# SSD decay built with log dt and a mask added on GpSimd, and projection slabs placed elsewhere, in a hybrid trunk layer

## Chip, cores and metric

One Trainium2 chip, one core. The metric is the device time of one execution of the whole layer, in microseconds, lower is better.

## The reference, cut to what matters

One layer over 256 context tokens and 1024 latent tokens of width 1024: modulated RMSNorm, an input projection whose columns go to three mixers (SSD, gated MLP, S5), an output projection, then a squared-ReLU MLP. The change touches the chunked SSD and the order of the projections:

```python
xbc = silu(conv5(s[..., XBC]))                 # columns x (512), B (2x128), C (2x128)
dt  = softplus(s[..., DT] + dt_bias)           # per direction and head
a_cum = cumsum(dt * a, chunk axis)             # chunks of 128 tokens
seg  = a_cum[q] - a_cum[k]
lmat = exp(where(k <= q, seg, -inf))           # reversed in the backward direction
y_diag = einsum(C[q] . B[k], lmat, x[k] * dt[k])
y_off  = einsum(C, h_prev, exp(a_cum))
h = chunk_decay * h + einsum(B, decay_to_end, x * dt)   # from chunk to chunk
y = y_fwd + y_bwd + d * x;   y = rmsnorm(y * silu(z))
```

## The kernel before, in words

Everything is float32 with channels on the partitions. Products with weights are done as three matmuls (`mm3`, L219 to L221) on high and low halves; a weight slab of 1024 x 128 (`wslab`) is loaded, split by ScalarE and VectorE, and multiplied with the token tiles of 256, 512 and 512 columns: 24 steps, 72 matmuls a slab. The slabs of interest: `xbc_slab(m)`, eight of them, each followed by a five-tap convolution (ScalarE's first tap, four `stt` on VectorE over 1284 columns, tanh, and a last multiplication on VectorE for m in 0, 1, 4, 6 and on GpSimd for the others) and stored to `xbc_d`; `u_slab`, two, a Gelu and a store issued from ScalarE's queue; `z_slab`, four, a Tanh, an `stt` and a store.

In the order of the source: input norm, the v/dt and S5 input projections, `sgu_mix`, two u slabs; then the S5 part, eight groups (`s5_main`), which holds five PSUM banks (`psA`); then xbc slabs 0, 1, 4, 6, `dt_chain`, and `psA.close()`. The SSD part takes the same banks as `psB`, so it starts when S5 is through. It has two head groups. `right()` walks the chunks from the last to the first and keeps the backward state of each (`hb`); `outputs()` walks forward over ten chunks. Group 0 needs slabs 0, 1, 4, 6; group 1 needs 2, 3, 5, 7, which stand between `right0` and `out0`. `right1` goes beside the last chunks of `out0`; z slabs 0 and 1 and `s5_glu` stand between `out0` and `out1`; z slabs 2 and 3, two `mixed_tile` and the first output slabs go beside `out1`.

A chunk of `outputs()` (L882 to L937): `rb`, the cumulated decay as rows for 4 heads and 2 directions, is broadcast from DRAM (three buffers); ScalarE makes `er = exp(rb)`; then the decay matrix is made head by head with pairs of a ScalarE and a VectorE instruction (`rb<-rb,col`), its minimum with the other direction and one Exp over 512 columns; `tok_major` transposes the chunk and C.B goes to `pcb`; VectorE masks `pcb` with both triangles (`cm`), four ScalarE and four VectorE instructions weigh it by dt (`rb<-cm,DTD`), and a VectorE product over 512 columns gives the operand of the matmuls at L918. State matmuls (L925) follow, `er`, `cm` and the store to `y_d` close the chunk, and `new_state` (L854) carries `hf` on.

The tile framework orders the instructions of each engine before the run with a planner: source order is the priority, and an instruction whose inputs and buffers are there may go ahead of earlier ones that are not ready. Each engine, and each DMA queue, then runs its list strictly in that order.

## Time and profile before

| what | value |
|---|---|
| median of 3 runs | 1580.24 us (1580.15 to 1582.12) |
| the profiled execution | 1578.67 us, span 1576.7 us |
| TensorE busy over the span | 1423.4 us (90%) |
| VectorE, ScalarE, GpSimd busy | 1067.9, 751.1, 389.5 us |
| granted TensorE clock, mean | 0.947 |

A granted clock of 1.00 is the upper level (2.4 GHz), 0.5 the lower (1.2 GHz); a mean between them is a mixture in time. Times of the rows are microseconds from the start of the span, durations of one instruction nanoseconds.

### The profile page before, as it was taken

What the parts mean: (1) busy time and instruction counts of PE and PEld (TensorE: products, weight loads), DVE (VectorE), ACT (ScalarE), POOL (GpSimd) and SP (SyncE); (2) the same over time, 40 slices, a digit from 0 to 9 for tenths busy, and PEclk for the clock granted to TensorE, in tenths of its full rate; (3) what the DMA queues carried; (4) which work ended last, traced back from release to release, by engine and by line L of the source; (5) the groups of instructions that cost most, each with busy time, mean ns of one, the idle gap of its engine ahead of it and who ended that gap; (6) DMA issues with size and microseconds to landing.
All of it is one profiled execution on the core that took longest, in us unless ns stands there. A gap on an engine that the chain in (4) does not pass through costs nothing.

```text
span 1576.7 us, 23817 instructions
## 1 busy us (share of the span) xinstructions
PE 1423.4 (90%) x8360; PEld 1202.6 (76%) x8360; DVE 1067.9 (68%) x1929; ACT 751.1 (48%) x1541; POOL 389.5 (25%) x487
## 2 busy tenths in 40 slices
PE   4689898999787779989999999999899999999795
PEld 3567676778565568878888888888788888887795
DVE  5773368668667885558977764674564768979945
ACT  3643434456645753437655554554555334424322
POOL 4555466613011122321100000000241313032033
PEclk9699999999997879999999999999999999999897
DMA  9759785264675647346444443344744245315312
GB/s 326 251 174 252 227 285 159 88 171 119 181 228 149 172 145 236 122 123 195 138 158 149 149 139 116 125 148 151 250 149 146 70 158 174 121 54 182 112 35 100
DMA packets 238903, 253.29 MB, mean 161 GB/s; under 512 B 15648, under 2 KB 163136, under 8 KB 238784
## 3 DMA queue, kind: packets, MB, share of 16 engines
q1 hardware_dynamic: 222880, 234.51, 48.2%
q10 hardware_dynamic: 15904, 17.27, 3.4%
q8 instruction: 66, 1.08, 0.3%
q14 instruction: 53, 0.43, 0.1%
HBM read 182.82 MB, written 68.89 MB: 160 GB/s over the span
## 4 chain that ended last, share of the span: by engine, by line
PE 58%; DVE 8%; DMA 6%; ACT 2%; issue 2%; POOL 1%; SPq 0%; DVEq 0%; ACTq 0%; POOLq 0%
PE ps_w L1215 7%; PE ps_w L1213 7%; PE ps_w L1214 7%; PE ps_w L1369 6%; PE ps_w L1370 6%; PE ps_w L1371 6%; PE ps_mm L219 4%; PE ps_mm L221 4%; PE ps_mm L220 4%; DMA rb<-rows_d 2%; PE ps_mm L1371 1%; PE ps_mm L1370 1%; PE ps_mm L1369 1%; DVE X L54 1%; DVE rb L57 1%
## 5 line engine op out<-in xcount | busy, mean ns | idle before, releaser
L219 PE MATMUL ps_mm<-hi,wh 128*128 128x512 f32 (+1 forms) x576 | 211.6, 367 | 20.1 <-DVE dtr L707 16.0
L221 PE MATMUL ps_mm<-hi,wl 128*128 128x512 f32 (+1 forms) x576 | 209.4, 364 | 0.9 <-DVE wl L54 0.9
L220 PE MATMUL ps_mm<-lo,wh 128*128 128x512 f32 (+1 forms) x576 | 209.8, 364 | 0.0
L1369 PE MATMUL ps_w<-uB,uA 128*128 128x512 f32 (+1 forms) x520 | 190.6, 371 | 9.3 <-ACT uB L60 8.9
L1370 PE MATMUL ps_w<-uB,uA 128*128 128x512 f32 (+1 forms) x520 | 191.3, 368 | 7.9 <-DVE uB L54 7.9
L1371 PE MATMUL ps_w<-uB,uA 128*128 128x512 f32 (+1 forms) x520 | 190.2, 367 | 0.0
L54 POOL TENSOR_TENSOR cb<-h 128x512 f32<-128x512 f32 x14 | 21.9, 1571 | 512.7 <-DMA h<-w 402.4
L219 PEld LDWEIGHTS ps_mm<-hi,wh 128*128 128x128 f32 x576 | 111.2, 193 | 38.1 <-DVE dtr L707 16.8
L221 PEld LDWEIGHTS ps_mm<-hi,wl 128*128 128x128 f32 x576 | 111.0, 193 | 18.1 <-DVE wl L54 1.8
L220 PEld LDWEIGHTS ps_mm<-lo,wh 128*128 128x128 f32 x576 | 111.0, 193 | 15.0 <-issue 0.6
L1369 PEld LDWEIGHTS ps_w<-uB,uA 128*128 128x128 f32 x520 | 99.9, 193 | 25.2 <-ACT uB L60 9.3
L1370 PEld LDWEIGHTS ps_w<-uB,uA 128*128 128x128 f32 x520 | 100.2, 193 | 24.7 <-DVE uB L54 9.8
L1371 PEld LDWEIGHTS ps_w<-uB,uA 128*128 128x128 f32 x520 | 99.8, 192 | 15.5
L60 ACT ACTIVATE uB<-tb 128x512 fp32r<-128x512 f32 x106 | 65.9, 625 | 64.9 <-PE ps_w L1371 31.7
L54 DVE TENSOR_TENSOR uB<-tb,uB 128x512 fp32r<-128x512 f32 x106 | 87.6, 846 | 13.1 <-ACT uB L60 13.1
L54 DVE TENSOR_TENSOR X<-X,ps_w 128x512 f32<-128x512 f32 x84 | 56.1, 680 | 27.7 <-PE ps_w L1371 27.6
L54 DVE TENSOR_TENSOR q<-q,ps_w 128x512 f32<-128x512 f32 x48 | 32.9, 685 | 59.7 <-PE ps_w L1215 59.0
L54 DVE TENSOR_TENSOR wl<-wraw,wh 128x1024 fp32r<-128x1024 f32 x32 | 48.4, 1514 | 36.7 <-ACT wh L60 35.9
L60 ACT ACTIVATE c<-c 128x512 f32<-128x512 f32 x64 | 40.3, 629 | 57.8 <-DVE c L54 56.9
L1371 PE MATMUL ps_mm<-ch,uA 128*128 128x256 f32 x224 | 63.2, 283 | 0.0
L1370 PE MATMUL ps_mm<-cl,uA 128*128 128x256 f32 x224 | 63.2, 283 | 0.0
L1369 PE MATMUL ps_mm<-ch,uA 128*128 128x256 f32 x224 | 63.1, 283 | 0.0
(435 smaller groups left out, 3875.3 us busy)
## 6 DMA issues: line engine op xcount, KB each, us to landing
rw<-w SPq DMA_DIRECT2D x112, 256.0 KB
tb<-a_d SPq DMA_DIRECT2D x106, 256.0 KB
aw<-ada_w SPq DMA_DIRECT2D x64, 256.0 KB
h<-w SPq DMA_DIRECT2D x32, 512.0 KB
a_d<-t SPq DMA_DIRECT2D x42, 256.0 KB
rb<-rows_d SPq DMA_DIRECT2D x20, 512.0 KB
adaw<-ada_w SPq DMA_DIRECT2D x32, 256.0 KB
wraw<-w_out SPq DMA_DIRECT2D x16, 512.0 KB
```

The costliest lines, as they stand in the source:

```text
L54: eng.tensor_tensor(out=out, in0=a, in1=b, op=op)
L57: V.scalar_tensor_tensor(out=out, in0=a, scalar=sc, in1=b, op0=op0, op1=op1)
L60: S.activation(out=out, in_=in_, func=func, **kw)
L219: T.matmul(out, lhsT=wh(k), rhs=xh(k), start=(k == 0), stop=False)
L220: T.matmul(out, lhsT=wh(k), rhs=xl(k), start=False, stop=False)
L221: T.matmul(out, lhsT=wl(k), rhs=xh(k), start=False, stop=(k == nk - 1))
L1213: T.matmul(out, lhsT=wh, rhs=X[0][:, j, :], start=(j == 0), stop=False)
L1214: T.matmul(out, lhsT=wh, rhs=X[1][:, j, :], start=False, stop=False)
L1215: T.matmul(out, lhsT=wl, rhs=X[0][:, j, :], start=False, stop=(j == 3))
L1369: T.matmul(out, lhsT=wh, rhs=bh, start=start, stop=False)
L1370: T.matmul(out, lhsT=wh, rhs=bl, start=False, stop=False)
L1371: T.matmul(out, lhsT=wl, rhs=bh, start=False, stop=stop)
```

## The change

Per chunk, the decay and dt become one exponential for each direction: `col` holds log dt minus the cumulated decay, made once in `dt_chain`; a constant `cap` holds 0 inside the triangle and -1e30 outside. GpSimd adds `cap` to `rb` into a new tile `sg` (two instructions over 512 columns), ScalarE takes eight Exp with `col` as bias, VectorE adds the directions and multiplies with `pcb`. Gone are the eight pairs of ScalarE and VectorE instructions, the mask of `pcb`, the Exp over 512 columns and the product of the two halves. `rb` has two buffers instead of three, `sg` two, `cm` three instead of two and is taken later; the backward states of both groups share sixteen buffers instead of nine each.

In the source order, xbc slabs 0 and 1 take the place of the u slabs before S5; xbc slabs 4, 6, 2, 3 stand ahead of S5 groups 1, 3, 5, 7; only xbc slabs 5 and 7 are left between `right0` and `out0`; the u slabs follow chunks 2 and 4 and z slabs 0 and 1 chunks 6 and 8 of `out0`.

```diff
@@ dt_chain
-        S.copy(col[:, 0], pc[:, 0:80])
-        act(col[:, 1], pc[:, 80:160], ACT.Copy, scale=-1.0)
+        V.tensor_scalar(out=col, in0=DTD, scalar1=1e-37, scalar2=None, op0=ALU.max)
+        act(col, col, ACT.Ln)
+        fl = col.rearrange("p d c -> p (d c)")
+        tt(fl, fl, pc[:, 0:160], ALU.subtract)
@@ right
-            hb[0] = new_state(f"hb{g}", 9, 1, 1, px, bt, None, "hb")
+            hb[0] = new_state("hb", 16, 1, 1, px, bt, None, "hb")
...
@@ outputs
-                rb = pool.tile([128, 2, 4, 128], F32, tag="rb", name="rb", bufs=3)
+                rb = pool.tile([128, 2, 4, 128], F32, tag="rb", name="rb", bufs=2)
-                cf, cbk = scal(col, 0, c), scal(col, 1, c)
+                sg = pool.tile([128, 2, 4, 128], F32, tag="sg", name="sg", bufs=2)
+                for d in range(2):
+                    tt(sg[:, d], rb[:, d], cap[:, d].unsqueeze(1).to_broadcast([128, 4, 128]), ALU.add, G)
...
-                for hh in range(4):
-                    act(rb[:, 1, hh], rb[:, 1, hh], ACT.Identity, bias=cbk[:, hh:hh + 1])
-                    stt(rb[:, 1, hh], rb[:, 0, hh], cf[:, hh:hh + 1], rb[:, 1, hh], ALU.subtract, ALU.min)
-                act(rb[:, 1], rb[:, 1], ACT.Exp)
+                for d in range(2):
+                    cd = scal(col, d, c)
+                    for hh in range(4):
+                        act(sg[:, d, hh], sg[:, d, hh], ACT.Exp, bias=cd[:, hh:hh + 1])
+                tt(sg[:, 0], sg[:, 0], sg[:, 1], ALU.add)
...
-                cm = pool.tile([128, 2, 128], F32, tag="cm", name="cm", bufs=2)
-                tt(cm, pcb.unsqueeze(1).to_broadcast([128, 2, 128]), tri[:, 0:2], ALU.mult)
-                d0, d1 = scal(DTD, 0, c), scal(DTD, 1, c)
-                for hh in range(4):
-                    act(rb[:, 0, hh], cm[:, 0], ACT.Copy, scale=d0[:, hh:hh + 1])
-                    stt(rb[:, 0, hh], cm[:, 1], d1[:, hh:hh + 1], rb[:, 0, hh], ALU.mult, ALU.add)
-                tt(rb[:, 1], rb[:, 1], rb[:, 0], ALU.mult)
+                tt(sg[:, 0], pcb.unsqueeze(1).to_broadcast([128, 4, 128]), sg[:, 0], ALU.mult)
@@ the order of the stages
-        for m in range(2):
-            u_slab(m)
+        for m in (0, 1):
+            xbc_slab(m)
...
+            if gp % 2:
+                xbc_slab((4, 6, 2, 3)[gp // 2])
             cur = s5_main(p5m, gp, s5zm)
...
-    for m in (0, 1, 4, 6):
-        xbc_slab(m)
     dt_chain()
...
         drain(right0)
-        for m in (2, 3, 5, 7):
+        for m in (5, 7):
             xbc_slab(m)
         for c, _ in enumerate(out0):
+            if c in (2, 4):
+                u_slab(c // 2 - 1)
+            if c in (6, 8):
+                z_slab(c // 2 - 3, z_weights(c // 2 - 3), (0, 1, 2))
             if c >= 5:
                 next(right1, None)
                 next(right1, None)
         drain(right1)
-        for m in (0, 1):
-            z_slab(m, z_weights(m), (0, 1, 2))
         s5_glu()
```

## Rows read from the trace of the kernel before

**Rows 1.** The page: busy time by engine, and the granted clock in 40 slices.
```profile
PE 1423.4 (90%) x8360; PEld 1202.6 (76%) x8360; DVE 1067.9 (68%) x1929; ACT 751.1 (48%) x1541; POOL 389.5 (25%) x487
PEclk9699999999997879999999999999999999999897
```

**Rows 2.** Sums by stretch: PE, PEld, DVE, ACT, POOL busy, clock, DMA share, GB/s.
```profile
175.00:205.00 30.00, 29.85 (x172) 25.39 (x172) 5.16 (x15) 8.46 (x18) 5.95 (x10) 1.00 0.77 242
205.00:317.00 112.00, 103.97 (x745) 83.56 (x741) 86.11 (x147) 44.98 (x114) 74.11 (x99) 0.97 0.53 166
317.00:413.00 96.00, 89.99 (x498) 75.68 (x497) 67.98 (x104) 61.39 (x111) 23.42 (x24) 1.00 0.57 161
413.00:455.00 42.00, 34.23 (x181) 25.20 (x180) 26.61 (x70) 21.48 (x54) 5.37 (x8) 0.92 0.79 225
455.00:525.00 70.00, 49.44 (x239) 37.15 (x239) 50.76 (x140) 40.44 (x114) 15.30 (x22) 0.75 0.60 149
525.00:575.00 50.00, 34.75 (x167) 28.21 (x168) 41.19 (x104) 35.78 (x86) 9.71 (x11) 0.74 0.59 166
575.00:592.00 17.00, 17.00 (x110) 14.63 (x110) 14.71 (x28) 6.68 (x11) 2.72 (x2) 0.97 0.42 130
```

**Rows 3.** Waits between 413 and 575: total us, times, longest.
```profile
ACT er L60 <- DMA rb<-rows_d: 23.6, 9, 5.3
PE ps_ws L854 <- DVE xw L54: 23.4, 8, 4.7
```

**Rows 4.** By tile: min/median/max ns, first and last start; S5's last matmuls, the chunks' first.
```profile
L637 PE MATMUL ps_w<-Ht,Y x64: 297/300/404, 206.0 to 317.3; 128*128 128x161 f32 x64
L904 PE MATMUL ps_wa<-xc x40: 270/275/583, 378.8 to 565.8; 128*128 128x128 f32 x40
L918 PE MATMUL ps_wb<-rb,xs x160: 272/323/476, 389.7 to 589.5; 128*64 128x128 f32 x160
```

**Rows 5.** First step of the slab matmuls by stretch, and S5's share between 175 and 205.
```profile
175.00:205.00 30.00, 17.14 (x48) 9.01 (x48) 1.00 0.77 242
205.00:317.00 112.00, 40.64 (x112) 21.20 (x112) 0.97 0.53 166
...
L592 PE MATMUL ps_w<-u,XT 128*64 128x163 f32 x26 | 2.2, 308 | 0.1
```

**Rows 6.** Tiles rb, cm and er: the instructions of a chunk.
```profile
L60 ACT ACTIVATE rb<-rb,col x80: 384/388/406, 333.5 to 567.1; 128x128 f32<-128x128 f32 x80
L57 DVE SCALAR_TENSOR_TENSOR rb<-rb,col x80: 324/347/1315, 333.9 to 568.6; 128x128 f32<-128x128 f32 x80
L60 ACT ACTIVATE rb<-cm,DTD x80: 384/388/406, 381.4 to 573.7; 128x128 f32<-128x128 f32 x80
L57 DVE SCALAR_TENSOR_TENSOR rb<-cm,DTD,rb x80: 334/344/837, 383.1 to 575.3; 128x128 f32<-128x128 f32 x80
L60 ACT ACTIVATE rb<-rb x20: 612/630/635, 338.5 to 571.8; 128x512 f32<-128x512 f32 x20
L54 DVE TENSOR_TENSOR rb<-rb x20: 673/682/1511, 386.2 to 576.2; 128x512 f32<-128x512 f32 x20
...
L54 DVE TENSOR_TENSOR cm<-ps_wa,pk x20: 411/418/426, 380.9 to 571.9; 128x256 f32<-128x256 f32 x20
...
L54 DVE TENSOR_TENSOR er<-ps_wb,er x20: 409/682/692, 391.7 to 591.4; 128x512 f32<-128x512 f32 x16, 128x256 f32<-128x256 f32 x4
```

**Rows 7.** GpSimd's two-input instructions between 317 and 592.
```profile
L54 POOL TENSOR_TENSOR sq<-sq,z x7: 723/1265/2058, 473.4 to 590.0; 128x512 f32<-128x512 f32 x4, 128x256 f32<-128x256 f32 x3
```

**Rows 8.** Order of time, VectorE and GpSimd around 345.
```profile
345.61 3.11 DVE L54 TENSOR_TENSOR wl<-wraw,wh 128x1024 fp32r<-128x1024 f32 x1 [3.33 <-ACT wh L60]
...
344.71 2.93 POOL L54 TENSOR_TENSOR xbc<-xr,xbc 128x1284 f32<-128x1284 f32 x1 [3.02 <-ACT xr L60]
```

**Rows 9.** Tiles wraw and xr: the undisturbed split, and one convolution tap.
```profile
L54 DVE TENSOR_TENSOR wl<-wraw,wh x32: 1208/1226/3110, 58.3 to 687.3; 128x1024 fp32r<-128x1024 f32 x32
...
L57 DVE SCALAR_TENSOR_TENSOR xbc<-xr,cwh,xbc x32: 1540/1556/2008, 231.7 to 386.8; 128x1284 f32<-128x1284 f32 x32
```

**Rows 10.** Groups by line between 317 and 592: ScalarE's table loads.
```profile
L60 ACT ACT_TABLE_LOAD x8 | 10.3, 1283 | 3.8 <-DMA rb<-rows_d 2.3 <-DMA yf<-y_d 1.4
```

More of the change, by code (lines that the diff above doesn't have):

```diff
@@ L825, in xbc_slab, with ssd_group @@
         load(xbc_d[g, a], acc)
-    def ssd_group(pool, g):
+    def ssd_group(pool, g, cap):
         hb = {1: None}
@@ L875, in right @@
             load(O["ssdo"][:, 512 + g * 256:512 + (g + 1) * 256], hbf)
-            hb[9] = init(1, f"hb{g}", 9)
+            hb[9] = init(1, "hb", 16)
             yield
@@ L879, in right @@
                 px, bt, _ = tok_major(chunk_xbc(c, 3))
-                hb[c - 1] = new_state(f"hb{g}", 9, 1, c, px, bt, hb[c], "hb")
+                hb[c - 1] = new_state("hb", 16, 1, c, px, bt, hb[c], "hb")
                 yield
@@ L917, in outputs @@
                     for par in range(2):
-                        T.matmul(py[par * 64:(par + 1) * 64, a, :], lhsT=xs[:, 2 * a + par], rhs=rb[:, 1, 2 * a + par],
+                        T.matmul(py[par * 64:(par + 1) * 64, a, :], lhsT=xs[:, 2 * a + par], rhs=sg[:, 0, 2 * a + par],
                                  start=True, stop=True)
@@ L927, in outputs @@
                 tt(er[:, ds], po[:, ds], er[:, ds], ALU.mult)
+                cm = pool.tile([128, 2, 128], F32, tag="cm", name="cm", bufs=3)
                 for a in range(2):
@@ L1076, in trunk_kernel @@
     with tc.tile_pool(name="pd", bufs=1) as pd, banks("psB"):
-        (right0, out0), (right1, out1) = [ssd_group(pd, g) for g in range(2)]
+        cap = pd.tile([128, 2, 128], F32, name="cap")
+        V.tensor_scalar(out=cap, in0=tri[:, 0:2], scalar1=-1.0, scalar2=1e30, op0=ALU.add, op1=ALU.mult)
+        (right0, out0), (right1, out1) = [ssd_group(pd, g, cap) for g in range(2)]
         def drain(g):
```

## The prediction

> **What bounds the kernel now.** I read the page first. TensorE is busy 90% of the span [rows 1], so the kernel as a whole is bound by it, and a change can win only where TensorE waits or runs at the lower clock. The clock line shows where that is: apart from the start, the digits 7, 8, 7 stand at slices 13 to 15, that is from about 470 to 590 us. Second, the sums by stretch [rows 2], which the reader should go through for TensorE's column and the clock. From 175 to 413 it is nearly full: 29.85 of 30, 103.97 of 112, 89.99 of 96. From 413 to 575 it is not: it idles 42 - 34.23 = 7.8, 70 - 49.44 = 20.6 and 50 - 34.75 = 15.3 us, 43.6 together, and what it does runs at a mean clock of 0.92, 0.75, 0.74. This is the SSD part after the slabs that served as filling are used up. Busy time times clock estimates the work at the upper level from 317 to 592: 90.0 + 31.5 + 37.1 + 25.7 + 16.5 = 200.8 us in a stretch of 275. If TensorE never paused, the last chunk's matmuls, now at 589.5 [rows 4], could stand at 317 + 201 = 518: 71 us are the most that this change can bring. No other engine is full there: from 317 to 592 VectorE sums to 201, ScalarE to 166, GpSimd to 57 us [rows 2]. So a chain with waits sets the pace. Third, the waits of 413 to 575 [rows 3]: ScalarE waits 23.6 us for `rb` to land, and TensorE 23.4 us for `xw`, which stands in VectorE's list behind the decay instructions of the chunk. Fourth, where the chain starts: S5's last matmuls are at 317.3, the first chunk's C.B at 378.8, its L918 at 389.7, the last chunk's at 589.5 [rows 4]. Twenty chunks, 19 steps: (589.5 - 389.7)/19 = 10.5 us a chunk.
>
> **The change part by part.**
>
> *Slabs before the chunks.* Between 175 and 205 the two u slabs run: 172 matmuls, of which 26 are S5's (2.2 us) and two more are others, so 144, two slabs, in about 27.4 us [rows 2, 5]. Their place goes to xbc slabs 0 and 1. In the S5 stretch the first of the three matmul steps runs 112 times, 24 to a slab: 4.7 slabs [rows 5]. These are 0, 1, 4, 6 and most of 2: the planner already fills S5 with slabs that the source puts behind it. With two slabs done before, the same TensorE time gets through 4, 6, 2, 3 and part of 5. What is ahead of `out0` on TensorE shrinks by two slabs and its first chunk starts 27.4 us sooner; the u slabs come back later as filling for pauses. That is a gain only while the chunk chain and not TensorE's sum sets the end: the end at 589.5 may come down to 518, so 27.4 fits. I count -27.4.
>
> *What the moved slabs do to S5.* Four slabs now stand ahead of S5 groups in the priority, not behind them. Each brings four taps of 1.556 us to VectorE [rows 9], 6.2 us, which is 86.11 of 112 us busy there already [rows 2]; an S5 group's products queue behind a tap. S5's end frees the banks of the SSD part, so a later end moves all chunks. Bounds: 0, because 4.7 slabs share that stretch now already, and 4 x 6.2 = 25 us if S5 waits for every tap. A gain is left out, since TensorE, near full there, has no less to do. Halfway, +12.
>
> *The chunk.* VectorE loses 4 x 0.347 + 4 x 0.344 + 0.418 + 0.682 = 3.86 us and gets a sum and a product over 512 columns, 2 x 0.682 (the second reads PSUM, as `er<-ps_wb,er` does): 1.36. Net -2.50 us a chunk, 50 us in all [rows 6]. ScalarE keeps eight instructions of 128 columns at 0.388 and loses the 0.630 Exp: -0.63. GpSimd gets two additions over 512 columns; the nearest row has 1.265 us as its median and 2.058 as its longest [rows 7]: 2.53 us a chunk, up to 4.1. GpSimd is busy 57 of 275 us, so 51 to 82 more fit, but its list now has the additions ahead of the `hf` and `hb` products and of `er<-er`, for which the next state and the chunk's store wait.
>
> *The port.* The 128x1024 split takes 1.226 us undisturbed; the one that starts at 345.61, while GpSimd multiplies from 344.71 to 347.64, takes 3.11 and ends just behind it [rows 8, 9]. So a VectorE instruction with two SBUF inputs waits for the GpSimd one. With 2.53 us of additions in some 9 us a chunk, such an instruction meets one with a chance of about 0.28, and waits up to 1.27 us; of four to five such instructions a chunk, 0.3 to 1.6 us come back on VectorE. The Trainium skill, GPSIMD Engine Reference, "Engine selection", advises VectorE for elementwise sums on a tile, calling GpSimd about twice as slow with two inputs, and "Specifications" calls the SBUF interfaces shared with VectorE. It speaks against this move; the trace agrees on both (1.265 against 0.682 us, and the stalled split). If it decides, the time is again that of the first rival.
>
> *ScalarE's tables.* The u slabs' six Gelus now lie among Exps: at up to two loads each, 12 x 1.283 = 15.4 us [rows 10]. ScalarE, 166 of 275 us busy, covers them if they fall into its pauses; if they fall on the chain it is 15.4/19 = 0.8 us a chunk. The new Ln in `dt_chain` may add a load or two, beside S5 work. The Trainium skill, ScalarE: Activation LUTs, "Table sets: the hidden batching unit", says to finish all calls of one set before switching, and puts a switch at about 2.66 us with its drain. By that figure it would be an estimated 32 us, 1.7 a chunk, and the time that of the first rival below; no row shows the drain as a gap.
>
> *Buffers.* `rb` is held from its issue to L918 with three buffers now; afterwards only until `er` and the two additions are done, so two buffers give loads earlier and most of the 23.6 us wait [rows 3] should go. `cm` no longer waits for an old store early in the chunk.
>
> What all this gives per chunk: the bounds are +0.8 us (tables on the chain, nothing gained) and -2.5 us (VectorE's net in full). VectorE is not the only thing in the chain, and the port gives part back: I take -1.0, which lies near what is left of 2.5 after the port's larger end, 0.9. 19 x 1.0 = -19.
>
> **Sum.** -27.4 + 12 - 19 = -34.4. The profiled execution takes 1578.67 us, 1576.7 of it span; it becomes 1544.3. The median shown is 1.57 us above the profiled one, so 1545.9. The forecast's own range, from both ends of the terms that I hold likely (S5 0 to 25, chunk 0 to -2.0): 1515 to 1578, with its middle between 1530 and 1560.
>
> **The rivals.**
> - *Order alone.* GpSimd's additions, the port and the table loads eat the chunk's gain; the chain stays at 10.5 us. For it: the larger port estimate plus 0.8 for tables is 2.4, all of the 2.5. Against: ScalarE's 23.6 us wait for `rb` has its own remedy. 1578.67 - 27.4 + 12 = 1563.3, so about 1565.
> - *TensorE full to the end.* The pace falls so far that only TensorE's sum counts: -71, 1509. For it: no engine but TensorE is full in that stretch [rows 2], and VectorE gets 50 us lighter. Against: two mixed tiles and the fewer slabs left beside `out1`.
> - *S5 late, and slower.* The planner gives slabs 4, 6, 2, 3 TensorE and VectorE ahead of S5 groups 1, 3, 5, 7, and S5 waits for each slab's whole TensorE time, 13.7 us: its end moves by 55 from 317. It decides from a delay of 27.4 + 19 = 46 us on. Then 1578.67 + 55 - 46 = 1587, about 1589. For it: S5 is a chain of TensorE, VectorE and GpSimd in turn. Against: a slab needs `wraw`, `xr` and `xb` buffers, two each, which spread it.
> - *Nothing.* The planner runs slabs wherever they fit already (4.7 in S5), so the new source order changes little, and the removed instructions lay under waits: 1580.
>
> **How the numbers follow.** Forecast 0.45, order alone 0.22, TensorE full 0.10, S5 late 0.15, nothing 0.08. About 0.2% (3 us) is what a measurement here can tell from no change. Faster: 0.45 + 0.22 + 0.10 = 0.77; same 0.08; slower 0.15. The range leaves out the slower case (0.15) and the lowest part of the full TensorE (0.05): 1512 to 1582.
>
> **What would show it.** Right: C.B of the first chunk near 352 instead of 378.8 and S5's last matmuls no later than 330; L918 steps near 9.5 us; the wait of `er` for `rb` mostly gone; TensorE's idle time from S5's end to the last chunk well under 44 us with the clock near 1. Wrong: S5's end beyond 350; GpSimd's additions above 2 us and VectorE's two-input instructions stretched by as much; more than 16 table loads in the SSD part with ScalarE as the last releaser of L918; or the time lost again behind the chunks, where mixed tiles and output slabs start sooner and meet other loads.

## The result, and the profile after

The changed kernel takes 1569.58 us (median; 1566.57 to 1572.70), the kernel before 1581.18 us beside it: a ratio of 0.9926 [0.9905, 0.9948], about 11.6 us faster. The forecast had the direction, and its range holds the time, but of its 34 us a third came. The profiled execution takes 1566.57 us, 1564.8 of it span, against 1576.7 before: 11.9 us less.

The page of the changed kernel, busy time by engine and the granted clock (before: [rows 1]):

```profile
PE 1413.3 (90%) x8360; PEld 1196.2 (76%) x8360; DVE 1055.0 (67%) x1772; ACT 743.3 (48%) x1521; POOL 446.9 (29%) x527
PEclk9799899999999889999999999999999999999897
```

The number of matmuls is the same, 8360. TensorE's idle time has hardly moved: 1576.7 - 1423.4 = 153.3 us before, 1564.8 - 1413.3 = 151.5 after. What fell is the time the same matmuls take, by 10.1 us. Busy time times the mean granted clock of the span gives the same work for both: 1423.4 x 0.947 = 1348.0 and 1413.3 x 0.954 = 1348.3. So the matmuls are not less work, they ran at the upper level for a larger part of their time. These are single executions, and the four of the changed kernel have spans from 1564.8 to 1570.9 us at mean clocks of 0.950 to 0.954: a split into idle time and clock is good to a few us.

The sums by stretch of the changed kernel, in the stretches and columns of [rows 2]:

```profile
175.00:205.00 30.00, 30.00 (x180) 25.29 (x176) 10.97 (x17) 9.44 (x15) 1.94 (x6) 1.00 0.83 264
205.00:317.00 112.00, 100.38 (x734) 81.99 (x733) 100.33 (x154) 50.34 (x113) 78.69 (x97) 0.97 0.51 159
317.00:413.00 96.00, 86.52 (x456) 72.65 (x456) 43.38 (x52) 50.33 (x92) 31.78 (x32) 0.96 0.50 150
413.00:455.00 42.00, 38.24 (x213) 28.60 (x210) 30.62 (x57) 26.71 (x74) 20.90 (x20) 0.96 0.77 214
455.00:525.00 70.00, 49.48 (x299) 39.21 (x298) 46.40 (x94) 43.67 (x122) 36.49 (x39) 0.90 0.74 200
525.00:575.00 50.00, 36.63 (x226) 30.40 (x225) 41.32 (x73) 30.04 (x71) 24.47 (x21) 0.83 0.57 171
```

The digits 7, 8, 7 of the clock line are 9, 8, 8 now, and the mean clock of 455 to 525 went from 0.75 to 0.90. TensorE still idles 20.5 us there, as before (20.6), and in 317 to 413 it now idles 9.5 us where it idled 6.0.

By tile, S5's last matmuls and the chunks' instructions of the changed kernel (minimum, median, longest in ns, first and last start; before: [rows 4, 6, 7]):

```profile
L637 PE MATMUL ps_w<-Ht,Y x64: 297/299/637, 223.8 to 332.4; 128*128 128x161 f32 x64
L911 PE MATMUL ps_wa<-xc x40: 270/275/377, 403.3 to 553.0; 128*128 128x128 f32 x40
L918 PE MATMUL ps_wb<-sg,xs x160: 272/273/477, 406.8 to 560.1; 128*64 128x128 f32 x160
L54 POOL TENSOR_TENSOR sg<-rb,cap x40: 1257/1287/2520, 348.2 to 549.2; 128x512 f32<-128x512 f32 x40
```

S5 starts 17.8 us later and ends 15.1 later; the first C.B comes at 403.3, 24.5 us later than before; the step from chunk to chunk is (560.1 - 406.8)/19 = 8.07 us instead of 10.5; the last chunk's matmuls start 29.4 us sooner. From there to the end of the span it is 1004.7 us instead of 987.2.

Now both spans cut at these marks (S5's last matmul, first C.B, last L918). The columns are those of [rows 2]. The kernel before:

```profile
0.00:317.30 317.30, 258.38 (x2093) 210.28 (x2094) 196.86 (x470) 138.20 (x341) 176.10 (x305) 0.92 0.70 219
317.30:378.80 61.50, 58.66 (x320) 50.02 (x319) 40.91 (x47) 34.67 (x60) 18.30 (x20) 1.00 0.51 143
378.80:589.50 210.70, 163.95 (x858) 128.44 (x856) 157.56 (x391) 130.41 (x314) 36.25 (x47) 0.84 0.64 175
589.50:1576.70 987.20, 942.37 (x5099) 813.86 (x5095) 672.59 (x1023) 447.85 (x829) 158.87 (x116) 0.98 0.44 140
```

The changed kernel:

```profile
0.00:332.40 332.40, 271.40 (x2156) 222.37 (x2157) 225.36 (x483) 152.21 (x352) 189.59 (x316) 0.92 0.67 211
332.40:403.30 70.90, 61.42 (x305) 50.85 (x304) 28.86 (x33) 35.05 (x59) 17.27 (x14) 0.95 0.56 170
403.30:560.10 156.80, 121.60 (x718) 95.33 (x718) 113.82 (x214) 101.56 (x271) 82.58 (x80) 0.90 0.69 192
560.10:1564.80 1004.70, 958.86 (x5190) 827.68 (x5186) 686.95 (x1043) 454.51 (x841) 157.43 (x118) 0.97 0.44 140
```

These eight lines hold the whole result, if each stretch is split into busy and idle time of TensorE:

- Ahead of the first C.B: +24.5 us. 48 matmuls more (2461 against 2413) and 15.8 us more busy time; 8.7 us more idle time, 6.6 of it between S5's end and the first C.B.
- Among the chunks: -53.9 us, of which only 11.6 are idle time saved (46.8 to 35.2). The other 42.3 are busy time: 140 matmuls fewer ran there, at a better clock.
- Behind the last chunk: +17.5 us, 16.5 of it busy time: 91 of those matmuls run here now.

So most of what the shorter chunk stretch seems to win is work that now runs elsewhere. How many slab steps ran in each stretch is in the matmuls of L219 alone (time, busy and count of matmuls, the same of weight loads, clock, DMA share, GB/s). The kernel before:

```profile
0.00:317.30 317.30, 101.73 (x288) 56.41 (x288) 0.92 0.70 219
317.30:378.80 61.50, 32.11 (x89) 16.78 (x89) 1.00 0.51 143
378.80:589.50 210.70, 42.04 (x113) 22.31 (x112) 0.84 0.64 175
```

The changed kernel:

```profile
0.00:332.40 332.40, 110.47 (x309) 61.49 (x309) 0.92 0.67 211
332.40:403.30 70.90, 32.23 (x84) 16.55 (x84) 0.95 0.56 170
403.30:560.10 156.80, 26.77 (x71) 13.90 (x71) 0.90 0.69 192
```

Ahead of the first C.B stood 288 + 89 = 377 steps, and now stand 309 + 84 = 393 (in both, 80 of them are S5's input projection and not slabs). Not one slab has left that place. The next two lines (by tile; the second of 380 to 460) say which they are: the u slabs are evicted from 355.1 to 387.8, and the first z slab's tiles at 390.7, 396.9 and 403.9. Their matmuls run ahead of the first C.B, although the source has these slabs behind chunks 2, 4 and 6.

```profile
L60 ACT ACTIVATE ue<-ps_mm x6: 383/578/599, 355.1 to 387.8; 128x512 f32<-128x512 f32 x4, 128x256 f32<-128x256 f32 x2
L60 ACT ACTIVATE ze<-ps_mm x8: 383/576/607, 390.7 to 457.6; 128x512 f32<-128x512 f32 x5, 128x256 f32<-128x256 f32 x3
```

Before, the first tile of a z slab (eight steps, evicted at 378.7) ran at that point; now all 24 steps do. That is the difference of 16.

The waits of the changed kernel: TensorE between S5's end and the first C.B (one line), then 413 to 575 (three lines; before: [rows 3]); total us, times, longest:

```profile
PE ps_mm L219 <- ACT ue L60: 7.8, 3, 4.7
...
PE ps_wb L918 <- ACT xs L914: 18.5, 7, 6.4
PE ps_ws L857 <- DVE xw L54: 2.5, 3, 1.0
ACT er L60 <- DMA rb<-rows_d: 2.9, 1, 2.9
```

Both waits of [rows 3] are gone: 23.6 to 2.9 for `rb`, 23.4 to 2.5 for `xw`. In the place of the second stands the wait for `xs` and the product behind the eight Exps. The 7.8 us are new: the u slabs' next tile waits until ScalarE has evicted the one before.

### The profile page after: what moved, and what is told of

The parts are those of the page before. It is cut to its first block, busy times and chain, and to the rows that moved or that the text cites. A ratio compares the mean times of both kernels' runs of the same rounds, so it can differ in the third digit from the quotient of the medians.

```text
span 1564.8 us, 23687 instructions
## 1 busy us (share of the span) xinstructions
PE 1413.3 (90%) x8360; PEld 1196.2 (76%) x8360; DVE 1055.0 (67%) x1772; ACT 743.3 (48%) x1521; POOL 446.9 (29%) x527
## 4 chain that ended last, share of the span: by engine, by line
PE 60%; DVE 10%; ACT 4%; DMA 4%; issue 4%; POOL 3%; SPq 0%; DVEq 0%; ACTq 0%; POOLq 0%
PE ps_w L1220 7%; PE ps_w L1218 7%; PE ps_w L1219 7%; PE ps_w L1374 6%; PE ps_w L1375 6%; PE ps_w L1376 6%; PE ps_mm L221 5%; PE ps_mm L219 5%; PE ps_mm L220 5%; PE ps_mm L1375 1%; PE ps_mm L1376 1%; PE ps_mm L1374 1%; DVE X L54 1%; DMA z<-z_d 1%; DVE uA L54 1%
## 5 line engine op out<-in xcount | busy, mean ns | idle before, releaser
L219 PE MATMUL ps_mm<-hi,wh 128*128 128x512 f32 (+1 forms) x576 | 213.6, 371 | 22.6 <-DVE dtr L707 13.3
L221 PE MATMUL ps_mm<-hi,wl 128*128 128x512 f32 (+1 forms) x576 | 210.3, 365 | 1.7 <-DVE wl L54 1.7
L54 POOL TENSOR_TENSOR cb<-h 128x512 f32<-128x512 f32 x14 | 22.3, 1599 | 516.1 <-DMA h<-w 403.7
L219 PEld LDWEIGHTS ps_mm<-hi,wh 128*128 128x128 f32 x576 | 112.5, 195 | 41.2 <-DVE dtr L707 14.2
L221 PEld LDWEIGHTS ps_mm<-hi,wl 128*128 128x128 f32 x576 | 112.2, 195 | 18.7 <-DVE wl L54 2.8
L220 PEld LDWEIGHTS ps_mm<-lo,wh 128*128 128x128 f32 x576 | 112.7, 196 | 15.8 <-issue 0.8
L54 DVE TENSOR_TENSOR uB<-tb,uB 128x512 fp32r<-128x512 f32 x106 | 86.9, 839 | 12.6 <-ACT uB L60 12.6
L54 DVE TENSOR_TENSOR wl<-wraw,wh 128x1024 fp32r<-128x1024 f32 x32 | 49.6, 1551 | 36.3 <-ACT wh L60 36.1
L54 POOL TENSOR_TENSOR sg<-rb,cap 128x512 f32<-128x512 f32 x40 | 56.2, 1427 | 32.8 <-PE ps_wb L918 23.0
L1376 PE MATMUL ps_mm<-ch,uA 128*128 128x256 f32 x224 | 63.2, 283 | 0.0
```

The lines of the kernel that those rows point to most:

```text
L54: eng.tensor_tensor(out=out, in0=a, in1=b, op=op)
L219: T.matmul(out, lhsT=wh(k), rhs=xh(k), start=(k == 0), stop=False)
L220: T.matmul(out, lhsT=wh(k), rhs=xl(k), start=False, stop=False)
L221: T.matmul(out, lhsT=wl(k), rhs=xh(k), start=False, stop=(k == nk - 1))
L1376: T.matmul(out, lhsT=wl, rhs=bh, start=False, stop=stop)
```

## The experiments

All ratios are to the kernel before, with 95% intervals. A code cut is against the kernel that the text names; those of e1 and e2 are against the changed kernel. Two theories stood at the start: the new arithmetic of the chunk brings the gain and the new order of slabs costs; or the order brings it, as forecast, and something else eats it.

**The two halves apart.** e1 has the new arithmetic and buffers, with the slabs where they were:

```diff
-        for m in (0, 1):
-            xbc_slab(m)
+        for m in range(2):
+            u_slab(m)
...
-            if gp % 2:
-                xbc_slab((4, 6, 2, 3)[gp // 2])
...
+    for m in (0, 1, 4, 6):
+        xbc_slab(m)
     dt_chain()
...
-        for m in (5, 7):
+        for m in (2, 3, 5, 7):
             xbc_slab(m)
         for c, _ in enumerate(out0):
-            if c in (2, 4):
-                u_slab(c // 2 - 1)
-            if c in (6, 8):
-                z_slab(c // 2 - 3, z_weights(c // 2 - 3), (0, 1, 2))
...
+        for m in (0, 1):
+            z_slab(m, z_weights(m), (0, 1, 2))
```

> The new chunk arithmetic and buffers alone; every slab stands where it stood before the change. Theory 'pace' (the gain is the chunk's shorter chain, the moved slabs cost): S5 ends at 317 again, the first C.B comes near 379, the steps of L918 stay near 8.0 us, and the time is that of the changed kernel or below, 1558 to 1570. Theory 'order' (the gain is the slabs as filling, which keep the clock up): most of the gain is gone, 1576 to 1581.

Measured: 1555.21 us, 0.9853 [0.9830, 0.9875], 23 us faster than before and the best median of all. e2 is the other half, the new order with the old arithmetic (cut to the decay's first lines):

```diff
-                for d in range(2):
-                    tt(sg[:, d], rb[:, d], cap[:, d].unsqueeze(1).to_broadcast([128, 4, 128]), ALU.add, G)
+                for hh in range(4):
+                    act(rb[:, 1, hh], rb[:, 1, hh], ACT.Identity, bias=cbk[:, hh:hh + 1])
+                    stt(rb[:, 1, hh], rb[:, 0, hh], cf[:, hh:hh + 1], rb[:, 1, hh], ALU.subtract, ALU.min)
...
```

> The new place of the slabs alone, with the chunk's arithmetic and buffers of before. Theory 'pace': S5 ends near 332, the first C.B near 400, steps of L918 near 10.5 us, and the time is not below before: 1580 to 1595. Theory 'order': 1569 to 1574.

Measured: 1598.23 us, 1.0121 [1.0102, 1.0141], 19 to 20 us slower than before. Both spans, cut at their own marks, e1 first:

```profile
0.00:316.90 316.90, 256.27 (x2089) 209.48 (x2090) 196.72 (x471) 137.94 (x339) 175.96 (x305) 0.92 0.69 219
316.90:379.70 62.80, 60.18 (x324) 50.69 (x323) 40.85 (x39) 34.77 (x61) 23.25 (x24) 1.00 0.52 147
379.70:546.10 166.40, 142.84 (x765) 111.31 (x765) 115.72 (x218) 109.01 (x277) 88.65 (x81) 0.86 0.69 201
546.10:1553.40 1007.30, 957.24 (x5190) 826.08 (x5186) 690.54 (x1046) 456.61 (x842) 162.65 (x118) 0.98 0.44 140
```

and e2:

```profile
0.00:332.30 332.30, 273.43 (x2157) 223.57 (x2158) 223.41 (x482) 149.71 (x351) 191.13 (x316) 0.92 0.67 211
332.30:404.10 71.80, 63.22 (x303) 51.91 (x302) 28.78 (x41) 35.47 (x58) 12.14 (x10) 0.90 0.55 160
404.10:602.20 198.10, 145.13 (x784) 114.06 (x782) 146.07 (x375) 115.90 (x299) 33.35 (x45) 0.80 0.58 164
602.20:1596.30 994.10, 948.99 (x5126) 818.13 (x5120) 680.87 (x1033) 451.12 (x834) 160.01 (x116) 0.98 0.44 140
```

The new order delays the first C.B by the same amount with either arithmetic (378.8 to 404.1; 379.7 to 403.3), and it costs idle time in the same two places with either. Between S5's end and the first C.B it is 2.8 to 8.6 us with the old arithmetic and 2.6 to 9.5 with the new; among the chunks 46.8 to 53.0, and 23.6 to 35.2. The arithmetic alone takes the idle time among the chunks from 46.8 to 23.6 us. Over e1's whole span 16.4 us of idle time and 6.9 us of busy time are gone (5.3 us of idle time come back behind the chunks), and that is its gain of 23. The two kernels also show the arithmetic's worth at nearly the same filling: among the chunks 88 slab steps of L219 run in e1 and 87 in e2 (e1 first), and the step is 8.44 us in e1 and 9.90 in e2.

```profile
379.70:546.10 166.40, 33.95 (x88) 16.99 (x87) 0.86 0.69 201
404.10:602.20 198.10, 31.16 (x87) 16.84 (x87) 0.80 0.58 164
```

TensorE's longest wait among the chunks of e1 is the one that the changed kernel has at 18.5 us:

```profile
PE ps_wb L918 <- ACT xs L914: 11.0, 7, 2.6
```

The first theory stands: the order gives back 11 to 14 of the 23 us.

**The additions' engine.** e4 is the changed kernel with the mask's additions on VectorE:

```diff
-                    tt(sg[:, d], rb[:, d], cap[:, d].unsqueeze(1).to_broadcast([128, 4, 128]), ALU.add, G)
+                    tt(sg[:, d], rb[:, d], cap[:, d].unsqueeze(1).to_broadcast([128, 4, 128]), ALU.add)
```

> The changed kernel with the two additions of the mask on VectorE instead of GpSimd. Theory 'port' (GpSimd's additions hold up VectorE by as much as they spare it): VectorE has 2 x 0.69 us more a chunk but no stretched instructions, the steps of L918 stay within 0.4 us of 8.0 and the time within 3 us of 1569.6. Rival (the additions are free on GpSimd): steps up to 1.4 us longer, 8.5 to 9.4, and 8 to 15 us more, 1577 to 1585.

Measured: 1570.67 us, 0.9943 [0.9926, 0.9961]; the interval overlaps with that of the changed kernel. Its page, its additions by tile, and its sums from S5's end to the first C.B and from there to the last chunk:

```profile
PE 1425.9 (91%) x8360; PEld 1206.7 (77%) x8360; DVE 1060.6 (68%) x1812; ACT 743.9 (47%) x1521; POOL 393.1 (25%) x487
...
L54 DVE TENSOR_TENSOR sg<-rb,cap x40: 674/685/1207, 346.9 to 550.1; 128x512 f32<-128x512 f32 x40
...
331.40:401.40 70.00, 61.75 (x304) 51.67 (x304) 27.59 (x37) 35.19 (x59) 10.84 (x10) 0.93 0.60 173
401.40:561.20 159.80, 128.69 (x720) 101.11 (x718) 123.59 (x250) 101.38 (x270) 36.62 (x45) 0.85 0.67 189
```

VectorE gets 40 additions with a median of 0.685 us, 28.5 us busy in all. But in these two stretches, where the additions run, its busy time is 27.59 + 123.59 = 151.2 us against 28.86 + 113.82 = 142.7 in the changed kernel, only 8.5 more. The other 20.0 us I read as the time by which GpSimd's additions had stretched VectorE's instructions, since nothing else was changed in the source: 1.0 us a chunk, inside the 0.3 to 1.6 of the forecast. One such instruction shows it: the sum `cm<-cm,er`, with both inputs in SBUF, has a median of 0.593 us in the changed kernel and of 0.417 in e4. So these additions spare VectorE about 0.4 us a chunk where they are. The step is 8.23 us in e4 and 8.07 in the changed kernel.

**Which part of the order costs.** e3 is the changed kernel with slabs 4, 6, 2, 3 behind S5 instead of among its groups.

```diff
-            if gp % 2:
-                xbc_slab((4, 6, 2, 3)[gp // 2])
...
+    for m in (4, 6, 2, 3):
+        xbc_slab(m)
     dt_chain()
```

> The changed kernel with slabs 4, 6, 2, 3 behind the S5 groups in the source again, not among them; slabs 0 and 1 stay ahead of S5. Theory 'S5 late' (the 15 us by which S5 ends later move all chunks): S5's end comes back to 317 to 323, the first C.B to 385 to 390, and the time falls by 5 to 10 us to 1560 to 1565. Rival (the first chunk waits for the backward walk and not for S5): S5 ends sooner, the first C.B stays near 400, time 1567 to 1572.

Measured: 1564.17 us, 0.9907 [0.9886, 0.9928]; S5 ends at 329.6 instead of 332.4. A few us at most; the intervals overlap. In the trace the edit moves little: 299 steps of L219 run up to S5's end instead of 309, so most of what the source now has behind S5 still runs inside it. e6 goes from e1, not from the changed kernel: xbc slabs 0 and 1 in the u slabs' place, the u slabs behind `right1` with the z slabs.

```diff
-        for m in range(2):
-            u_slab(m)
+        for m in (0, 1):
+            xbc_slab(m)
...
-    for m in (0, 1, 4, 6):
+    for m in (4, 6):
         xbc_slab(m)
...
         for m in (0, 1):
+            u_slab(m)
             z_slab(m, z_weights(m), (0, 1, 2))
```

> The new arithmetic with the old order, but for one exchange: slabs 0 and 1 stand ahead of S5 and the u slabs behind out0 with z slabs 0 and 1. Theory 'convolutions ahead of S5' (their VectorE taps hold up S5's first groups, and all behind S5 with them): S5's first output matmul comes near 223 instead of 206, the first C.B near 395 to 403, and the time is 8 to 12 us above that of the arithmetic alone, 1563 to 1568. Rival (the loss lies with the slabs among the S5 groups and in out0): within 3 us of 1555.

Measured: 1586.94 us, 1.0033 [1.0019, 1.0047]: this swap costs 28 to 32 us (by the ratios, by the medians), all that e1 had gained and more, and far above what either reading expected. S5 ends at 332.4 and the first C.B is at 403.7, as in the changed kernel. e11 is e3 with the u and z slabs behind `out0` and `right1`:

```diff
         for c, _ in enumerate(out0):
-            if c in (2, 4):
-                u_slab(c // 2 - 1)
-            if c in (6, 8):
-                z_slab(c // 2 - 3, z_weights(c // 2 - 3), (0, 1, 2))
...
         drain(right1)
+        for m in (0, 1):
+            u_slab(m)
+            z_slab(m, z_weights(m), (0, 1, 2))
```

> The kernel of e3_s5free with u slabs 0 and 1 and z slabs 0 and 1 behind out0 and the second backward walk in the source, not among the chunks. It differs from e6_swap only in slabs 2 and 3, which stand ahead of dt_chain. If the place of the u slabs in the source gives back what the exchange costs: the time rises from 1564 to 1580 or more. If slabs 2 and 3 ahead of the SSD part do: it stays within 4 us of 1564.

Measured: 1583.65 us, 1.0009 [0.9998, 1.0020], 16 to 19 us more than e3. So u and z slabs among the chunks of `out0` give back more than half of what the swap ahead of S5 costs; the change's repair is real, but it repairs damage of its own. e12 keeps the u slabs ahead of S5 and makes the rest of the new order behind S5:

```diff
-    for m in (0, 1, 4, 6):
+    for m in (0, 1, 4, 6, 2, 3):
         xbc_slab(m)
...
-        for m in (2, 3, 5, 7):
+        for m in (5, 7):
             xbc_slab(m)
         for c, _ in enumerate(out0):
+            if c in (6, 8):
+                z_slab(c // 2 - 3, z_weights(c // 2 - 3), (0, 1, 2))
```

> The new arithmetic with the u slabs ahead of S5, as before the change, slabs 0, 1, 4, 6, 2, 3 behind S5, only 5 and 7 between right0 and out0, and z slabs 0 and 1 behind chunks 6 and 8. If slabs 2 and 3 ahead of dt_chain are worth something by themselves: 1540 to 1550, below the arithmetic alone. If they only repair what the exchange of the u slabs broke: within 4 us of 1555.

Measured: 1564.69 us, 0.9892 [0.9875, 0.9910], 6 to 9 us more than e1, which neither reading expected. S5 ends at 320.3, but the first C.B is at 397.3: more slab work ahead of the chunks costs here too, with S5 nearly untouched.

**Why S5 comes late.** The forecast had blamed the convolutions' taps on VectorE. e10 is e6 with the convolution of slabs 0 and 1 (not their matmuls) behind S5:

```diff
-        for m in (0, 1):
-            xbc_slab(m)
+        xr01 = [xbc_proj(m) for m in (0, 1)]
...
+    for m in (0, 1):
+        xbc_conv(m, xr01[m])
```

> The kernel of e6_swap, in which only the matmuls of slabs 0 and 1 stay ahead of S5; their convolution (first tap, four VectorE taps, tanh, product, store) stands behind S5 in the source. Theory 'taps' (VectorE's taps hold up S5's first groups): S5's first output matmul comes back from 224 to below 212 and the time from 1587 to 1555 to 1570. Rival (S5 starts late because of what stands before it on the DMA queue and on TensorE): S5's first output stays above 218 and the time above 1578.

Measured: 1586.47 us, 1.0024 [1.0013, 1.0035], the same as e6, with S5 from 223.5 to 333.2. But the edit did not move the taps in time. VectorE's first four, in e6 and then in e10:

```profile
194.02 6.33 DVE L57 SCALAR_TENSOR_TENSOR xbc<-xr,cwh,xbc 128x1284 f32<-128x1284 f32 x4 [0.74 <-ACT xbc L60]
194.18 6.33 DVE L57 SCALAR_TENSOR_TENSOR xbc<-xr,cwh,xbc 128x1284 f32<-128x1284 f32 x4 [0.74 <-ACT xbc L60]
```

The next four start at 208.9 to 217.7 in e6 and at 208.6 to 217.4 in e10. So e10 took no tap out of S5's way, and it leaves the theory untested. The changed kernel does have taps there: on VectorE three of them, 1.55 us each, lie between the first sum of S5's first group, at 207.7, and its scan, at 215.0; before, sum and scan stand at 193.3 and 195.1, with no tap between.

The next theory was SP's DMA queue: in the changed kernel seven loads of `aw` (for ada) stand at 176.6 to 184.8 us ahead of S5's `u` (187.8 instead of 184.0) and `XT` (190.9 instead of 187.2). e14 is e6 with the ada groups at S5's groups 1, 3, 5, meant to bring these loads later:

```diff
-            if gp in (0, 2, 4):
+            if gp in (1, 3, 5):
                 ada_group()
```

> The kernel of e6_swap with the three groups of the modulation product, whose weights are loaded on the same DMA queue as S5's inputs, in front of S5 groups 1, 3 and 5 instead of 0, 2 and 4. Theory 'queue' (in the exchanged order seven of those loads go ahead of S5's inputs and make S5 late): S5's first output matmul comes back from 224 to 206 to 214 and the time falls by 5 us or more, below 1582. Rival (VectorE's taps or TensorE's slab tiles): S5's first output stays above 218, time within 4 us of 1587.

Measured: 1573.06 us, 0.9944 [0.9928, 0.9961], 14 us less than e6; S5's last matmul is at 327.2, the first C.B at 391.6. But S5's first output comes at 225.0, no sooner than in e6, and the loads have not moved: `aw` from 177.1 to 185.0, `u` at 189.1, `XT` at 192.3. So the 14 us are real (TensorE idles 33.6 us among the chunks instead of 45.0), but not the queue's, and their cause is not shown. e15 and e16 put the same edit into the changed kernel and into e1.

> The changed kernel as it stands, with the three groups of ada moved from S5's groups 0, 2, 4 to 1, 3, 5. Theory (the aw loads stand in SP's queue ahead of S5's inputs once the u slabs no longer stand between them): S5's first L592 near 197 us instead of 206.9, the first C.B near 391 instead of 403.3, the step of the chunks still 8.0 to 8.2, the last chunk near 548; time near 1557 us, 12 less than the changed kernel. Rival (chunks that start sooner only run slower, as in the kernel whose chunks went ahead of the right side): the last chunk stays at 558 to 562, step near 8.7; 1566 to 1571.

> The new arithmetic with the old order of slabs, and the three groups of ada moved from S5's groups 0, 2, 4 to 1, 3, 5. Theory (in the old order S5's inputs are queued ahead of the aw loads already, so nothing is to be had): S5's first L592 at 192 as before, 1553 to 1558 us. Rival (the ada groups cost S5 and the chunks time wherever the slabs stand): S5 ends 5 us sooner, near 312, chunks as much sooner, 1541 to 1549 us.

Measured: e15 1565.10 us, 0.9896 [0.9877, 0.9916]; e16 1559.72 us, 0.9867 [0.9844, 0.9890]. S5's first step (L592) and its last (L637) in e15:

```profile
L592 PE MATMUL ps_w<-u,XT x128: 298/302/353, 194.9 to 307.1; 128*64 128x163 f32 x128
L637 PE MATMUL ps_w<-Ht,Y x64: 297/300/637, 225.1 to 334.2; 128*128 128x161 f32 x64
```

Six of the seven `aw` loads and S5's first `XT` on SP's queue, in the changed kernel:

```profile
177.93 6.85 SPq L48 DMA_DIRECT2D aw<-ada_w  x6
190.94 0.44 SPq L48 DMA_DIRECT2D XT<-xt_d  x1
```

The same in e15, and S5's first 16 products on TensorE there:

```profile
177.41 6.27 SPq L48 DMA_DIRECT2D aw<-ada_w  x6
190.91 0.43 SPq L48 DMA_DIRECT2D XT<-xt_d  x1
...
194.95 0.46 PE L592 MATMUL ps_w<-u,XT 128*64 128x163 f32 x2 [1.52 <-DMA XT<-xt_d]
206.44 1.33 PE L592 MATMUL ps_w<-u,XT 128*64 128x163 f32 x14
```

The loads have not moved here either, so no run tests the queue theory by its edit. These rows speak against it all the same. In e15 two products start as soon as `XT` has landed, at 194.95, and the other 14 come at 206.44, as late as in the changed kernel (206.87). There `XT` is issued at the same time, TensorE is busy for 15.00 of the 15.00 us from 192 to 207 with slab steps and ada's products, and L592 waits 0.5 us for loads in all. So S5's first products stand behind that work in TensorE's list; the loads do not hold them. S5 ends at 334.2 in e15, no sooner, and the first C.B is at 405.1. In time e15 gains 4 to 5 us at most, at the edge of the intervals, not the 14 of e14, and in e16 the edit gains nothing.

What e15 shares with the changed kernel is the count of slab matmuls (L219 to L221, without the 240 of S5's input projection): 686 up to S5's end and 939 up to the first C.B, in both. e14, where S5 did end sooner, has 616 and 869, e6 657 and 925. Over the runs the first C.B goes with that count: 889 in before and e1 (378.8, 379.7), 864 in e16 (381.7), 873 in e7 (381.3), 919 to 925 in e3, e6, e10, e11 and e12 (397.3 to 403.7), 939 in e2, e15 and the changed kernel (403.3 to 405.1). e14 is away from the line, 10 us late. The count alone proves no cause, since a late S5 also leaves more time in which slabs are run. For the stretch behind S5's end e8 (below) decides it, by keeping slabs out: with 14 steps of L219 there instead of 84 it takes 39.5 us instead of 70.9. So TensorE's own slab work holds the first chunk back there; for S5's own late start it is shown only that TensorE is full.

**Is the start of the chunks worth anything?** The -27.4 us rest on it. e7 (from e1) moves slabs 2, 3, 5, 7 behind the first four chunks:

```diff
-        for m in (2, 3, 5, 7):
-            xbc_slab(m)
         for c, _ in enumerate(out0):
+            if c < 4:
+                xbc_slab((2, 3, 5, 7)[c])
```

> The new arithmetic with the old order, but slabs 2, 3, 5, 7 stand behind chunks 0 to 3 of out0 in the source and not ahead of it. Theory 'priority' (four slabs ahead of out0 hold its chunks back): the first C.B comes 20 us or more before 379.7 and the time falls by 5 to 15 us below 1555. Rival (the first chunks wait for the backward walk, which has priority over both): the first C.B stays within 8 us of 379.7 and the time within 3 us of 1555.

Measured: 1563.43 us, 0.9885 [0.9865, 0.9906]; the first C.B is at 381.3, no sooner than in e1, and the time is 5 to 8 us longer. With the slabs taken out of the way on paper, the backward walk `right0` still stands ahead of `out0`, and slabs run in its pauses. e9 (from e1) therefore puts two steps of `right0` and two chunks first:

```diff
+        next(right0)
+        next(right0)
+        for _ in range(2):
+            next(out0)
         drain(right0)
-        for m in (2, 3, 5, 7):
+        for m in (2, 3):
             xbc_slab(m)
-        for c, _ in enumerate(out0):
+        for c, _ in enumerate(out0, 2):
+            if c < 4:
+                xbc_slab((5, 7)[c - 2])
```

> The new arithmetic with the old order, but the first two steps of the backward walk are followed in the source by chunks 0 and 1 of out0, then the rest of the walk, slabs 2 and 3, and slabs 5 and 7 behind chunks 2 and 3. If the chunks wait for the walk's priority: the first C.B comes to 345 to 360, the steps of L918 get longer at first, and the time falls by 5 to 15 us below 1555. If the pace of the whole chain counts and not its start: within 4 us of 1555.

Measured: 1558.97 us, 0.9865 [0.9837, 0.9893], the same as e1. Its chunks and its L219 in the stretch from the first C.B to the last chunk:

```profile
L918 PE MATMUL ps_wb<-sg,xs x160: 272/273/477, 350.7 to 542.3; 128*64 128x128 f32 x160
...
343.60:542.30 198.70, 52.83 (x144) 27.53 (x144) 0.93 0.67 190
```

The chunks start 36 us sooner than in e1, 343.6 against 379.7, and end 3.8 us sooner: the step grew from 8.44 to 10.08 us, and 144 slab steps instead of 88 now run among them. An earlier start alone gives nothing where the slabs it passes must still run. The remaining idea was that the changed kernel spends its filling too soon; e8 holds each u and z slab's weights back until a chunk is done (a VectorE copy of one column of that chunk's output into the weight buffer, before the load):

```diff
+        if gate is not None:
+            V.tensor_copy(out=raw[:, 0, 0:1], in_=gate)
         load(raw, src.rearrange("(k p) m -> p k m", p=128), eng)
...
-                u_slab(c // 2 - 1)
+                u_slab(c // 2 - 1, done[0])
```

> The changed kernel, with the weight load of u slabs 0 and 1 and z slabs 0 and 1 made to wait for the output of chunks 2, 4, 6 and 8 of out0 by a one-column VectorE copy into its buffer, so that the planner cannot run them sooner than the source has them. Theory 'filling spent too soon' (they run at 350 to 413 and are missed among the chunks): first C.B near 375, TensorE's idle time between 455 and 575 falls from 25 to below 15 us, and the time falls to 1552 to 1562. Rival (when the filling runs is all the same, since the chunks' chain sets the end): TensorE idles more ahead of the chunks, and the time is 1566 to 1580.

Measured: 1609.62 us, 1.0177 [1.0156, 1.0198], 40 us worse than the changed kernel. The first C.B does come at 370.5, but the step is 10.94 us and the last chunk at 580.1. Slabs forced among the chunks delay them (144 steps there instead of 71), and of the 39.5 us between S5's end and the first C.B TensorE idles 13.6. In this form the idea is refuted, but its price is not: of the 31.5 us by which TensorE idles longer than in the changed kernel, 22.9 lie behind the last chunk, 16.7 of them in a single wait (L200 for `sq` from GpSimd).

## Why the prediction came out as it did

**The order, -27.4: the step that failed.** It says that what is ahead of `out0` on TensorE shrinks by two slabs. It grew by 16 of a slab's 24 steps. The two counts it rested on were right: 48 steps of L219 before 205 and about 112 in the S5 stretch are 48 and 110 after. What it left out stands in its own rival "Nothing": the planner runs any slab that is ready in a pause, whatever its place in the source. After S5's end the backward walk is such a chain with pauses, and the u slabs, 355 to 388, went into them. The first C.B came 24.5 us later instead of some 15 sooner; with slabs kept out of those pauses by force (e8) it comes at 370.5. And e9 shows that even a start 36 us sooner would not have been worth its distance.

**S5, +12.** S5's end moved by 15.1. The size was near, but +12 was only the middle of two bounds, and the reason given for it is not confirmed. The first outputs (L637) start 17.8 us later (206.0 to 223.8). Of this, 14.9 lie ahead of S5's first products (192.0 to 206.9), where TensorE is full of slab steps and ada's products and doesn't wait for loads; the forecast priced VectorE's taps and not this. From the first product to the first output it is 16.9 us instead of 14.0; there taps do stand in VectorE's list, and what they cost is not shown, since e10 left them where they were. S5 itself ran no longer (111.3 to 108.6 us). e3 says little of the slabs among the groups, since it moved ten steps. Up to S5's end TensorE does 63 matmuls more, 13.0 of the 15.1 us; 2.1 are idle.

**The chunk, -19: right in direction, undersized.** The step fell by 10.52 - 8.07 = 2.45 us, 46.5 us over 19 steps, near the bound that has VectorE's net in full. But 71 slab steps instead of 113 now run among the chunks, so this is not the chain alone. At nearly the same filling (e2 against e1) it is 9.90 - 8.44 = 1.46 us, 28 us over 19 steps. The two waits that the forecast started from went from 23.6 to 2.9 us and from 23.4 to 2.5. All runs with the new arithmetic also have the new buffer counts, so how much is VectorE's lighter load and how much the buffers is not shown. The port took 1.0 us a chunk of VectorE's time (e4), inside the bounds; that the step pays for it is not seen: VectorE is busy 113.8 of the 156.8 us of the chunks. The advice in the Trainium skill, GPSIMD Engine Reference, "Engine selection", to keep elementwise sums on VectorE changes nothing in this kernel: with the sums on either engine the time is the same (e4), although one sum takes 1.287 us on GpSimd and 0.685 on VectorE. The table loads were no cost: 317 to 592 has nine where [rows 10] has eight.

**What no term held.** The sum lets the time end where the last chunk ends: +17.1 - 46.5 = -29.4 at the last L918. But 91 matmuls that used to run in the chunks' pauses run behind them, +17.5, and the net is -11.9. This was named among the signs of a wrong forecast and given no price. The bound of 71 us was built on TensorE's work, and the terms should have been too: its idle time and its clock are what an edit can win here, and of these 1.8 and 10.1 us came.

**The rivals.** "S5 late, and slower" had half of the mechanism: a later S5 and slab time ahead of the chunks, 24.5 us of it, with a chunk gain that outweighed it; e2, where that gain is missing, is slower. "Order alone" had the parts reversed. "TensorE full to the end" needed the idle time of the chunks to vanish; 35.2 of 46.8 us are left.

**The signs.** C.B near 352: 403.3. S5's end by 330: 332.4. Steps near 9.5: 8.07. `er`'s wait for `rb` gone: 2.9 of 23.6 left. TensorE's idle time from S5's end to the last chunk well under 44 us with the clock near 1: 9.5 + 35.2 = 44.7, between the same marks 49.6 before, and a clock of 0.95 and 0.90. Of the signs of a wrong forecast one came: the time lost behind the chunks.

**What stays open.** Why the swap ahead of S5 alone (e6) costs 28 to 32 us while the delay of the first C.B is the same as in the changed kernel is shown only in part: 30.3 us of it are idle time of TensorE against e1, 21.4 of them among the chunks, and the u and z slabs' place makes 16 to 19 us (e11 against e3). Why TensorE waits longer for `xs` among the chunks, 18.5 us against 11.0 in e1, is open too. The number of slab steps there (71 and 88) does not explain it: the idle time among the chunks is 28.5 us with 71 steps in e15, 34.2 with 96 in e16 and 45.0 with 76 in e6. e14's late C.B and its gain have no explanation, and what the taps cost S5 is untested. The lowest median is e1's, 1555.21 us: the new arithmetic without the new order.

## What to carry to other kernels

Where a planner fills pauses with any work that is ready, a new source order doesn't remove work from a place: count the filling steps that really run ahead of the chain, in the trace, before pricing a move. The same holds for an experiment: look in its trace whether the moved work has moved at all, before reading its time (the taps of e10 and the loads of e14 and e15 had not). Split each stretch between two marks into TensorE's busy and idle time; the idle time and the clock of the busy time are what can be won, and a chain that gets shorter pushes its filling to where it must be paid for. Try the two halves of a change alone: here one was worth 23 us and the other cost 19 to 20, or 11 to 14 on top of the first.

## What the runs showed of the hardware

Nearly all of the gain between the two profiled executions, 10.1 of 11.9 us, is the same 8360 matmuls taking less time at a mean granted clock of 0.90 among the chunks instead of 0.84, with TensorE's idle time the same within 2 us. Over the sixteen kernels of this case TensorE's busy time goes from 1410.9 us (e9, mean clock 0.957) to 1430.8 (e2, 0.941), by 1.4%, while busy time times mean clock stays within 0.5% (1345.9 to 1352.3). In e4 the clock works against it: TensorE idles 1570.0 - 1425.9 = 144.1 us, 7.4 less than in the changed kernel, its busy time is 12.6 us longer, and its profiled execution ends 5.2 us later. So a change of this kernel can save idle time and have about as much taken back by the clock.

A GpSimd addition whose two inputs lie in SBUF costs VectorE time as well: 40 of them, with a median of 1.287 us, stretched VectorE's instructions by about 20 us in all, seven tenths of the 28.5 us that VectorE needs to do them itself. This is worked out from e4 and the changed kernel, one execution of each.
